# A hybrid decoder layer: early products added by PE, sums by ACT and accumulating transfers, w_down's sums and the h reload moved

## The chip, the core and the metric

The kernel runs on one core of one Trainium2 chip. The metric is the device time of one execution in microseconds. All arithmetic is float32 to the caller; products go through PE as pairs of float32r numbers, a high part and a rest.

## What is computed

One decoder layer on 1024 tokens of width 1024: two token mixers (dilated-window attention and stick-breaking attention), gated and added, then cross-attention to 256 memory tokens, then a gated MLP with a width-3 convolution, then a norm. The change touches how the last parts are carried out.

```python
h = h + (gate_a * ya + gate_b * yb) @ w_out
h = h + memory_cross_attn(rms_norm(h), rms_norm(mem), w_xq, w_xkv, w_xo)
u = rms_norm(h) @ w_up                      # 1024 x 5632
u = causal_conv3(u) + conv_b
h = h + (silu(u[:, :2816]) * u[:, 2816:]) @ w_down
return rms_norm(h)
```

## The kernel before

Every matrix product takes three matmuls of 128x512 outputs (`mm3`, lines 97 to 99): high by high, high by rest, rest by high. A weight arrives raw by SP's queue (`raw_w`, line 70); ACT copies it to the high part (line 80) and DVE subtracts to get the rest (line 81).

The two large products of the MLP use a scheme with seven block products in place of eight. Tokens are cut in two halves (block column 1 is tokens 0 to 511), and the contraction in two halves. For `w_up`, `right_sums` (852) builds sums of the normed activations once (t1 to t4), and `sum_weights` (909) builds sums of the two weight blocks on DVE for each of 22 output tiles g. For each g the products add up in two PSUM banks, A and B. The results are put together as ug (gate) and uv (value), each a tile of 1026 columns: two leading zeros and 1024 tokens.

Two of the seven products, `11` and `21`, need only the first token half. For g under 10 (`NEARLY`) `up_early` (824) computes them beforehand, three of them between the second attention half and its output product, seven behind: p1 is the first product, c11 the sum of both; both are stored in DRAM (`e_d`). In the loop over g `up_start` (889) loads w_up's two tiles, p1, and c11 into ug; `up_middle` (925) and `up_end` (949) do the other five products and add p1 on DVE wherever it belongs:

```python
nc.vector.tensor_tensor(u["U2"], u["A"], u["p1"], op=ALU.add)                      # 936
nc.vector.tensor_tensor(u4, u["A"], u["p1"], op=ALU.add)                           # 944
nc.vector.tensor_tensor(u["uv"][:, 2 + HT:2 + T], u["B"], u4, op=ALU.add)          # 947
nc.vector.tensor_tensor(c12, u["A"], u["p1"], op=ALU.add)                          # 955
nc.vector.tensor_tensor(u["uv"][:, 2:2 + HT], u["B"], u["U2"], op=ALU.add)         # 959
```

For g from 10 on, all seven products are done in the loop, ACT copies p1, U2, U4 and c12 out of bank A, and DVE does the adds with bank D and bank B. Bank B holds t3's product at first, is read for the second half of uv, and goes on with t4's product for the first half. Then for ug and uv ACT starts y (965), DVE adds two convolution taps (966, 967), ACT applies silu, DVE multiplies (972), and for every second g DVE makes four sums (982 to 988). Seven tiles per pair go to DRAM as `r_d` from POOL's queue. ug and uv share two buffers (tag `hu`), so the tiles of one g become free only when the taps of the g before are done.

`down` (991) is the same scheme for `w_down`: seven runs of 11 steps kg, each with 12 matmuls and two loads of 256 KB on SP's queue (1014, 1015), one from `r_d`, one of a weight. Three of the runs take sums of weight blocks. These sums (`sd_d`) don't depend on the input activations; they are made in DRAM alone by `weight_sums` (512): for each of 11 pairs four copies of 256 KB on SP's queue (`put`, 516) and three accumulating transfers on POOL's queue (`add`, 519), each waiting for the one before. `sum_step` (533) issues them piece by piece; it is called in the loop over the merged gates (634), in `tok_gemm` (574), `feat_gemm` (733), `up_early` (825), `up_middle` (926) and `up_end` (950). h was stored to DRAM (`spill_h`, 836) to free its tiles, and `loads` (1001) reads it back after the first run of `down`, eight tiles of 512 KB and the gain gF on POOL's queue, into the tiles of ug, uv and y of the last outputs.

The order on each engine and queue comes from a scheduler, which goes by program order and by a simulated time line. `keep_in_program_order` pins a transfer to its place. Each engine and each queue then runs in that fixed order, and a waiting instruction holds all behind it.

Of the kernel before, what the change touches and what calls it, by code (L numbers as in the profile page):

```python
# [7 lines left out]
F32 = mybir.dt.float32  # L8
F32R = mybir.dt.float32r
AF = mybir.ActivationFunctionType  # L10
# [32 lines left out]
def hybrid_layer(ctx: ExitStack, tc: tile.TileContext, x, xT, mem, memT, w_in, w_v, w_br, w_out, w_xq, w_xk, w_xv, w_xo, w_up,  # L43
# [9 lines left out]
    vec = cp.tile([P, V_N], F32, name="vec")  # L53
    neghalf = cp.tile([P, 16], F32, name="neghalf")

    ga_d = dp.tile([16, P, T], F32, name="ga_d")
# [4 lines left out]
    r_d = dp.tile([NF // 2, 7, P, HT], F32, name="r_d")  # L61
    e_d = dp.tile([NEARLY, 2, P, HT], F32, name="e_d")
    h_d = dp.tile([8, P, D], F32, name="h_d")
# [98 lines left out]

    nc.sync.dma_start(ident, consts[:, 0:P])
    nc.sync.dma_start(cst, consts[:, P:])
    rs8 = ap.tile([P, 8], F32, name="rs8")
    for t in range(8):
# [14 lines left out]
    def load_rs_perm():  # L181
        rs_perm[4] = ap.tile([P, 16], F32, name="rs_p1")[:, 0:8]
        rs_perm[16] = ap.tile([P, 8], F32, name="rs_p2")
# [349 lines left out]
    def sum_step():  # L533
        n = sums_n[0]
        sums_n[0] += 1
        for b, ops in enumerate(sums):
            d = n - 15 * b // 2
            if 0 <= d < 12 and d % 2 == 0:
                ops[d // 2]()
# [5 lines left out]
    for p in range(NA + NS):  # L545
        units = [(dil_step, (8 * p + i,)) if p < NA else (sb_unit, (p, i)) for i in range(8)]
        if p == NA:
            units[CPOS:CPOS] = [(combine, (0,)), (combine, (1,))]
            units = [(dil_step, (8 * NA + i,)) for i in range(3)] + units
        gemms = [(fn, ()) for fn in proj_pair(p + 1)] if p + 1 < NA + NS else []  # L550
        ng = len(gates) if p == NA + NS - 1 else GATES[p]
        for _ in range(ng):
            gemms.append((gate, (gates.pop(0),)))
        nu, ngm = len(units), len(gemms)
        if p == NA + NS - 1:
            ngm = TAIL_MIX
        k = 0
        for u, (fn, a) in enumerate(units):
            while k < ngm and k * nu <= u * ngm:
                gemms[k][0](*gemms[k][1])  # L560
                k += 1
            fn(*a)
        while k < len(gemms):
            gemms[k][0](*gemms[k][1])
            k += 1
# [5 lines left out]
    def tok_gemm(th, ch, nkg, wdram, lhs, done):  # L571
        ps = quad("mmt")
        for kg in range(nkg):
            sum_step()
            ws = list(wchunks(wdram[ch, kg]))
            lh = [lhs(2 * kg + kk) for kk in range(2)]
            for t in range(4):
                ts_ = slice(t * P, (t + 1) * P)
                for kk in range(2):
                    lhi, llo = lh[kk]  # L580
                    mm3(ps[t], (lhi[:, ts_], llo[:, ts_]), ws[kk][1:], kg == 0 and kk == 0, kg == nkg - 1 and kk == 1)
        for t in range(4):
            done(4 * th + t, ch, ps[t])
# [80 lines left out]

    def etile(name):
        return ep.tile([P, HT], F32, tag="e", name=name, bufs=7)

# [16 lines left out]
    def mem_prep():  # L684
# [10 lines left out]
        rsm = xp.tile([P, 2], F32, name="rsm")  # L695
        for t in range(2):
# [35 lines left out]
    def feat_gemm(ps, dram, n2):  # L732
        sum_step()
        for k0, wh, wl in wchunks(dram):
            for kk in range(4):
                k, ks = k0 + kk, slice(kk * P, (kk + 1) * P)
                mm3(ps, (wh[:, ks], wl[:, ks]), (n2[0][:, k], n2[1][:, k]), k == 0, k == NK - 1)
# [85 lines left out]

    def up_early(g):
        sum_step()
        l11, l12 = gate_weights(g)
        pa, pb = bank("mm", 3, "pe"), bank("mm", 3, "pe")
        p1, c11 = etile("p1"), etile("c11")
        product(pa, l11, R["11"], True)
        nc.scalar.activation(p1, pa, AF.Copy)  # L830
        product(pb, l12, R["21"], True)
        nc.vector.tensor_tensor(c11, pb, p1, op=ALU.add)
        nc.gpsimd.dma_start(e_d[g, 0], p1)
        nc.gpsimd.dma_start(e_d[g, 1], c11)

# [53 lines left out]
    def up_start(g):  # L889
        u = {}  # L890
        u["ug"], u["uv"] = (htile([P, 2 + T + 14], "hu", n) for n in ("ug", "uv"))
        for n in ("ug", "uv"):
            nc.gpsimd.memset(u[n][:, 0:2], 0.0)
        u["A"] = bank("zz", 2, "pA")
        u["w1"] = raw_w(w_up[g])
        u["w2"] = htile([P, 2 * HT], "hr", "w2")
        nc.sync.dma_start(u["w2"], w_up[NF + g])
        u["p1"] = etile("p1")
        if g < NEARLY:
            nc.sync.dma_start(u["p1"], e_d[g, 0])  # L900
            nc.sync.dma_start(u["ug"][:, 2:2 + HT], e_d[g, 1])
        else:
            hi, lo = split(u["w1"])
            u["l12"] = hi[:, HT:], lo[:, HT:]
            product(u["A"], (hi[:, :HT], lo[:, :HT]), R["11"], True)
            nc.scalar.activation(u["p1"], u["A"], AF.Copy)
        return u

    def sum_weights(u):
# [15 lines left out]
    def up_middle(g, u):  # L925
        sum_step()
        early = g < NEARLY
        if not early:
            d = bank("mm", 3, "pD")
            product(d, u["l12"], R["21"], True)  # L930
            nc.vector.tensor_tensor(u["ug"][:, 2:2 + HT], d, u["p1"], op=ALU.add)
        s1, s2, s3, u["s4"] = sum_weights(u)
        product(u["A"], s2, R["t2"], early)
        u["U2"] = etile("U2")
        if early:
            nc.vector.tensor_tensor(u["U2"], u["A"], u["p1"], op=ALU.add)
        else:
            nc.scalar.activation(u["U2"], u["A"], AF.Copy)
# [4 lines left out]
        if early:  # L943
            nc.vector.tensor_tensor(u4, u["A"], u["p1"], op=ALU.add)  # L944
        else:
            nc.scalar.activation(u4, u["A"], AF.Copy)
        nc.vector.tensor_tensor(u["uv"][:, 2 + HT:2 + T], u["B"], u4, op=ALU.add)

    def up_end(g, u):
        sum_step()  # L950
        early = g < NEARLY
        product(u["A"], u["s4"], R["22"], False)
        c12 = u["ug"][:, 2 + HT:2 + T]
        if early:
            nc.vector.tensor_tensor(c12, u["A"], u["p1"], op=ALU.add)
        else:
            nc.scalar.activation(c12, u["A"], AF.Copy)
        product(u["B"], u["l22"], R["t4"], False)
        nc.vector.tensor_tensor(u["uv"][:, 2:2 + HT], u["B"], u["U2"], op=ALU.add)
        ys = []  # L960
# [30 lines left out]
    def down():  # L991
# [14 lines left out]
        def run(ps, i, first):  # L1006
            for kg in range(KG):
# [30 lines left out]

        run(A, 1, True)
        loads()  # L1040
        into(A, 0, 0, ALU.add)
        B = [bank("zz", 2, "dB") for _ in range(2)] + [bank("tr", 2, "dB") for _ in range(2)]
        run(B, 2, True)
        into(B, 0, 0, ALU.add, 0)
        run(A, 6, False)
        into(A, 0, 1, ALU.subtract)
        run(B, 7, True)
        into(B, 1, 1, ALU.subtract)
        run(A, 5, False)
        into(A, 1, 1, ALU.subtract, 0)  # L1050
# [21 lines left out]
    o1 = x_att(1, q1)  # L1072
    for g in range(3):
        up_early(g)
    xo_half(1, o1)
# [10 lines left out]
    ncw = mp.tile([P, 144], F32, name="ncw")  # L1086
    nc.vector.tensor_scalar(ncw[:, :3 * NF], vec[:, V_CW + 3 * NF:V_CW + 6 * NF], -1.0, None, op0=ALU.mult)
# [91 lines left out]
```

## Time and profile before

| what | us |
|---|---|
| median of 3 runs | 1793.84 |
| lowest and highest | 1786.63 and 1794.06 |
| the profiled execution | 1791.09 |
| its span in the trace | 1789.3 |
| busy PE, DVE, ACT, POOL | 1696.2, 1156.3, 823.3, 265.7 |

The stages in the span: projections and dilated attention to some 440 us, stick-breaking from there to 730, gates and merge to 840, `w_out` and cross-attention to 1090, early products and activation sums to 1157, the loop over g to 1548, then `down`. PE is the matmul engine, DVE the vector engine, ACT the scalar engine, POOL GpSimd, SP the engine that only issues transfers. A matmul's busy time in the trace is longer than its distance to the next one, since they overlap; the distance is what counts. The granted clock is the share of 2.4 GHz that PE was given.

### The profile page before, as it was taken

The numbers are of one execution on the slowest core, as the hardware profiler recorded it, in microseconds if no ns is written. First come the engines' busy times: TensorE is split into PE (matmuls) and PEld (weight loads), VectorE is DVE, ScalarE is ACT, GpSimd is POOL, SyncE is SP. The second block draws the span as 40 slices with busy tenths as digits, with TensorE's granted clock in tenths as the row PEclk, the third lists the DMA queues.
The fourth block names the chain that finished last, engine by engine and source line by source line (L and its number), as shares of the span: only waits on it lengthen the run. The fifth ranks groups of instructions, "written<-read, shape, count | busy, mean of one in ns | idle before, by whom it ended". The sixth has DMA issues, their size and how long they took to land.

```text
span 1789.3 us, 23340 instructions
## 1 busy us (share of the span) xinstructions
PE 1696.2 (95%) x8578; PEld 1377.3 (77%) x8578; DVE 1156.3 (65%) x1823; ACT 823.3 (46%) x1398; POOL 265.7 (15%) x434
## 2 busy tenths in 40 slices
PE   7999999998999999999899989799899999889996
PEld 5977777877878788787788777577688888668885
DVE  3664655367757566475545664999888788735556
ACT  5454554455345445344444454443344454424344
POOL 0442333211100000001100112111111111200002
PEclk9999999999999999999999999899999999989998
DMA  8443323323413122666652654566563432566663
GB/s 303 111 128 88 111 78 84 98 70 96 137 53 101 54 77 68 196 206 242 159 151 85 173 139 163 184 176 194 172 160 120 120 123 72 219 238 191 190 194 134
DMA packets 93650, 253.06 MB, mean 141 GB/s; under 512 B 14752, under 2 KB 15008, under 8 KB 93536
## 3 DMA queue, kind: packets, MB, share of 16 engines
q1 hardware_dynamic: 65360, 164.58, 28.5%
q0 software_dynamic: 28176, 86.99, 17.9%
q8 instruction: 67, 1.10, 0.3%
q14 instruction: 47, 0.39, 0.1%
HBM read 186.15 MB, written 71.67 MB: 144 GB/s over the span
## 4 chain that ended last, share of the span: by engine, by line
PE 40%; DVE 5%; DMA 4%; ACT 1%; issue 1%; POOL 1%; SPq 0%; POOLq 0%; DVEq 0%; ACTq 0%
PE pA L97 3%; PE pA L98 3%; PE pA L99 3%; PE dA L97 2%; PE dA L99 2%; PE dA L98 2%; PE mmt L97 2%; PE mmt L98 2%; PE dB L97 2%; PE mmt L99 2%; PE dB L99 2%; PE dB L98 2%; PE pB L98 2%; PE pB L97 2%; PE pB L99 2%; DMA sd_d<-in_w_down_dram 1%
## 5 line engine op out<-in xcount | busy, mean ns | idle before, releaser
L99 PE MATMUL mm<-a2h,wl 128*128 128x512 f32 x592 | 234.1, 396 | 0.0
L98 PE MATMUL mm<-a2l,wh 128*128 128x512 f32 x592 | 233.7, 395 | 0.0
L97 PE MATMUL mm<-a2h,wh 128*128 128x512 f32 x592 | 233.6, 395 | 0.0
L81 DVE TENSOR_TENSOR wl<-wr,wh 128x1024 fp32r<-128x1024 f32 (+1 forms) x119 | 145.2, 1221 | 91.2 <-ACT wh L80 90.8
L80 ACT ACTIVATE wh<-wr 128x1024 fp32r<-128x1024 f32 (+1 forms) x119 | 124.1, 1044 | 147.5 <-PE mmv L99 29.7
L81 DVE TENSOR_TENSOR dl<-rl,dh 128x1024 fp32r<-128x1024 f32 x77 | 94.2, 1223 | 94.7 <-ACT dh L80 91.0
L80 ACT ACTIVATE dh<-rl 128x1024 fp32r<-128x1024 f32 x77 | 81.5, 1059 | 124.9 <-PE dA L99 44.7
L98 PEld LDWEIGHTS mm<-a2l,wh 128*128 128x128 f32 x592 | 111.7, 189 | 22.2 <-issue 0.9
L99 PEld LDWEIGHTS mm<-a2h,wl 128*128 128x128 f32 x592 | 111.8, 189 | 22.0 <-issue 1.0
L97 PEld LDWEIGHTS mm<-a2h,wh 128*128 128x128 f32 x592 | 111.8, 189 | 21.8 <-issue 0.9
L490 DVE TENSOR_TENSOR_SCAN kp<-kp 128x128 f32<-128x128 f32 (+7 forms) x64 | 86.7, 1355 | 26.9 <-ACT kp L487 26.7
L487 ACT ACTIVATE kp<-zz,zsc 128x512 f32<-128x512 f32 (+3 forms) x96 | 55.6, 583 | 49.1 <-DVE zz L486 44.4
L378 ACT ACTIVATE sp<-sp,nm 128x128 f32<-128x128 f32 (+1 forms) x96 | 42.4, 442 | 73.1 <-DVE nm L376 73.0
L97 PE MATMUL pA<-a2h,mh 128*128 128x512 f32 x176 | 71.8, 408 | 3.2 <-DVE U L944 2.8
L499 ACT ACTIVATE at<-tra 128x512 f32<-128x512 f32 (+3 forms) x96 | 43.1, 489 | 68.6 <-PE tra L497 68.4
L97 PE MATMUL dA<-dh 128*128 128x512 f32 x176 | 63.3, 401 | 11.2 <-ACT dh L80 11.2
L98 PE MATMUL dA<-dl,dh 128*128 128x512 f32 x176 | 71.4, 406 | 1.8 <-DVE dl L81 1.8
L99 PE MATMUL dA<-dh,dl 128*128 128x512 f32 x176 | 71.2, 404 | 0.0
L98 PE MATMUL pA<-a2l,mh 128*128 128x512 f32 x176 | 70.9, 403 | 0.0
L99 PE MATMUL pA<-a2h,ml 128*128 128x512 f32 x176 | 70.6, 401 | 0.0
L110 POOL TENSOR_TENSOR ss<-ss,neghalf 128x1 f32<-128x1 f32 x24 | 25.1, 1124 | 254.7 <-DVE ss L593 253.6
L488 ACT ACTIVATE gg<-zz,zsc 128x512 f32<-128x512 f32 (+3 forms) x96 | 55.8, 583 | 6.8 <-DVE gg L491 6.7
(347 smaller groups left out, 4512.1 us busy)
## 6 DMA issues: line engine op xcount, KB each, us to landing
rl<-r_d SPq DMA_DIRECT2D x77, 256.0 KB, 2.7
wr<-in_w_in_dram SPq DMA_DIRECT2D x37, 512.0 KB, 3.9
wr<-in_w_up_dram SPq DMA_DIRECT2D x32, 512.0 KB, 4.5
w<-in_w_up_dram SPq DMA_DIRECT2D x22, 512.0 KB, 3.3
r_d<-ts POOLq DMA_DIRECT2D x44, 256.0 KB, 3.5
rl<-sd_d SPq DMA_DIRECT2D x44, 256.0 KB, 3.2
r_d<-y POOLq DMA_DIRECT2D x33, 256.0 KB, 3.8
rl<-in_w_down_dram SPq DMA_DIRECT2D x33, 256.0 KB, 3.1
```

The lines of the kernel that those rows point to most:

```text
L80: nc.scalar.activation(hi, raw, AF.Copy)
L81: nc.vector.tensor_tensor(lo, raw, f(hi), op=ALU.subtract)
L97: nc.tensor.matmul(ps, wh, rh, start=first, stop=False, **kw)
L98: nc.tensor.matmul(ps, wh, ro, start=False, stop=False, **kw)
L99: nc.tensor.matmul(ps, wo, rh, start=False, stop=last, **kw)
L110: nc.gpsimd.tensor_tensor(ss, ss, neghalf[:, :n], op=ALU.pow)
L378: nc.scalar.activation(sp[:, a, :n], sp[:, a, :n], AF.Exp, scale=0.125, bias=nm[:, a:a + 1], accum_out=ost[:, 130 + a:131 + a])
L487: nc.scalar.activation(kp[:, c0:c1], z[:, :n], AF.Sigmoid, scale=zsc[:, 1, i:i + 1])
L488: nc.scalar.activation(gg[:, c0:c1], z[:, :n], AF.Sigmoid, scale=zsc[:, 0, i:i + 1])
L490: nc.vector.tensor_tensor_scan(rev, rev, rev, 1.0, op0=ALU.mult, op1=ALU.bypass)
L499: nc.scalar.activation(s[:, :nb * P], tp[:, :nb * P], AF.Copy)
```

## The change

- `sum_step` is called in the units of the stick-breaking phase (pairs 6 to 9) and still in the merge loop, no longer in the later places. The sums of one pair start every 3 calls, before every 7.5.
- `up_early` takes two outputs at a time. The first product is stored as a high part and a rest (`er_d`, float32r) and the second product adds to it in the same PSUM bank; c11 is a copy of that bank by ACT. Two outputs are computed between the second attention half and its output product, eight behind.
- In the loop, for g under 10, the early product is loaded as its two parts by POOL's queue, and PE adds it into bank A with two matmuls by the identity. The adds of p1 on DVE are gone; U2, U4 and c12 are copies by ACT for all g.
- Bank B (and bank D) is copied into uv (ug) by ACT, and U4, U2 (p1) are added by an accumulating transfer from SBUF to SBUF on POOL's queue (`add_into`).
- The two leading zeros and the load of c11 move from `up_start` to `up_middle`.
- h is read back in quarters of four loads of 256 KB, on SP's queue, at kg 3 to 6 of four of the runs; gF in a fifth.
- Some small tiles get more columns.

```diff
+    ident_r = cp.tile([P, P + 16], F32R, name="ident_r")[:, :P]
...
-    e_d = dp.tile([NEARLY, 2, P, HT], F32, name="e_d")
+    e_d = dp.tile([NEARLY, P, HT], F32, name="e_d")
+    er_d = dp.tile([NEARLY, 2, P, HT], F32R, name="er_d")
...
+    nc.scalar.activation(ident_r, ident, AF.Copy)
...
-            d = n - 15 * b // 2
+            d = n - 3 * b
...
             fn(*a)
+            if p >= NA:
+                sum_step()
...
-            sum_step()
...
-    def up_early(g):
-        sum_step()
-        l11, l12 = gate_weights(g)
-        pa, pb = bank("mm", 3, "pe"), bank("mm", 3, "pe")
-        p1, c11 = etile("p1"), etile("c11")
-        product(pa, l11, R["11"], True)
-        nc.scalar.activation(p1, pa, AF.Copy)
-        product(pb, l12, R["21"], True)
-        nc.vector.tensor_tensor(c11, pb, p1, op=ALU.add)
-        nc.gpsimd.dma_start(e_d[g, 0], p1)
-        nc.gpsimd.dma_start(e_d[g, 1], c11)
+    def up_early(gs):
+        ps = {}
+        for g in gs:
+            ps[g] = bank("mm", 3, "pe"), *gate_weights(g)
+            product(ps[g][0], ps[g][1], R["11"], True)
+            hi, lo = etile("phi", F32R), etile("plo", F32R)
+            hilo(hi, lo, ps[g][0])
+            nc.gpsimd.dma_start(er_d[g, 0], hi)
+            nc.gpsimd.dma_start(er_d[g, 1], lo)
+        for g in gs:
+            product(ps[g][0], ps[g][2], R["21"], False)
+            c11 = etile("c11")
+            nc.scalar.activation(c11, ps[g][0], AF.Copy)
+            nc.gpsimd.dma_start(e_d[g], c11)
...
-        u["p1"] = etile("p1")
         if g < NEARLY:
-            nc.sync.dma_start(u["p1"], e_d[g, 0])
-            nc.sync.dma_start(u["ug"][:, 2:2 + HT], e_d[g, 1])
+            hi, lo = etile("phi", F32R), etile("plo", F32R)
+            nc.gpsimd.dma_start(hi, er_d[g, 0])
+            nc.gpsimd.dma_start(lo, er_d[g, 1])
+            nc.tensor.matmul(u["A"], ident_r, hi, start=True, stop=False, skip_group_check=True)
+            nc.tensor.matmul(u["A"], ident_r, lo, start=False, stop=True, skip_group_check=True)
...
+    def add_into(dst, ps, x):
+        nc.scalar.activation(dst, ps, AF.Copy)
+        nc.gpsimd.dma_start(dst, x, accum_op=ALU.add)
...
     def up_middle(g, u):
-        sum_step()
-        early = g < NEARLY
-        if not early:
+        for n in ("ug", "uv"):
+            nc.gpsimd.memset(u[n][:, 0:2], 0.0)
+        if g < NEARLY:
+            nc.sync.dma_start(u["ug"][:, 2:2 + HT], e_d[g])
+        else:
             d = bank("mm", 3, "pD")
             product(d, u["l12"], R["21"], True)
-            nc.vector.tensor_tensor(u["ug"][:, 2:2 + HT], d, u["p1"], op=ALU.add)
+            add_into(u["ug"][:, 2:2 + HT], d, u["p1"])
...
-        nc.vector.tensor_tensor(u["uv"][:, 2 + HT:2 + T], u["B"], u4, op=ALU.add)
+        nc.scalar.activation(u4, u["A"], AF.Copy)
+        add_into(u["uv"][:, 2 + HT:2 + T], u["B"], u4)
...
-        nc.vector.tensor_tensor(u["uv"][:, 2:2 + HT], u["B"], u["U2"], op=ALU.add)
+        add_into(u["uv"][:, 2:2 + HT], u["B"], u["U2"])
...
-        def loads():
-            nc.gpsimd.dma_start(gF, bass.AP(tensor=ln_f.tensor, offset=ln_f.offset, ap=[[0, P], [1, D]]))
-            for t in range(8):
-                tc.keep_in_program_order(nc.gpsimd.dma_start(h[t], h_d[t]))
+        def load_h(th, ch):
+            hs = slice(ch * HT, (ch + 1) * HT)
+            return [lambda t=t: nc.sync.dma_start(h[t][:, hs], h_d[t][:, hs]) for t in range(4 * th, 4 * th + 4)]
...
+                if kg >= 3 and kg - 3 < len(also):
+                    tc.keep_in_program_order(also[kg - 3]())
...
-    for g in range(3):
-        up_early(g)
+    up_early((0, 1))
...
-    for g in range(3, NEARLY):
-        up_early(g)
+    for g in range(2, NEARLY, 2):
+        up_early((g, g + 1))
```

## Rows read from the trace of the kernel before

**Rows 1.** The page, part 1: busy time, share and instructions of each engine.

```profile
PE 1696.2 (95%) x8578; PEld 1377.3 (77%) x8578; DVE 1156.3 (65%) x1823; ACT 823.3 (46%) x1398; POOL 265.7 (15%) x434
```

**Rows 2.** Stretches: span, busy (count) of PE/PEld/DVE/ACT/POOL, clock, DMA share, GB/s.

```profile
500.00:700.00 200.00, 200.00 (x1195) 160.28 (x1194) 129.05 (x161) 100.98 (x194) 10.14 (x19) 1.00 0.21 68
...
1139.00:1157.00 18.00, 9.60 (x30) 6.73 (x28) 16.37 (x21) 4.75 (x5) 1.69 (x4) 0.72 0.59 220
1157.00:1300.00 143.00, 129.63 (x529) 100.32 (x529) 130.50 (x159) 54.22 (x52) 23.10 (x51) 0.98 0.60 175
1300.00:1540.00 240.00, 240.00 (x1040) 195.21 (x1039) 198.89 (x225) 113.00 (x134) 32.09 (x76) 1.00 0.40 118
1546.00:1594.00 48.00, 34.98 (x125) 26.21 (x124) 23.11 (x22) 15.26 (x15) 7.49 (x14) 0.82 0.79 295
1600.00:1750.00 150.00, 150.00 (x658) 123.15 (x657) 80.25 (x85) 65.92 (x79) 0.57 (x1) 1.00 0.62 191
```

**Rows 3.** Waits of PE from 840 to 1300 us: total, times, longest.

```profile
PE pA L97 <- ACT mh L80: 16.4, 9, 6.1
PE pk L99 <- DVE wl L81: 6.0, 2, 5.2
```

**Rows 4.** Timeline of SP's queue and of DVE, 1270 to 1283 us.

```profile
1276.47 0.48 SPq L516 DMA_DIRECT2D sd_d<-sd_d  x1
1277.00 0.59 SPq L900 DMA_DIRECT2D p<-e_d  x1
...
1282.10 0.69 DVE L936 TENSOR_TENSOR U<-pA,p 128x512 f32<-128x512 f32 x1 [3.33 <-DMA p<-e_d]
```

**Rows 5.** The chain that ended last, 1545 to 1580 us: start, duration, what.

```profile
1550.63 1.29 DVE y L966
...
1552.19 9.34 DMA rl<-in_w_down_dram
...
1561.55 12.30 DMA rl<-in_w_down_dram
```

**Rows 6.** DMA issues of the whole run: transfer, queue, count, KB, median us to landing.

```profile
rl<-in_w_down_dram SPq DMA_DIRECT2D x33, 256.0 KB, 3.1
...
sd_d<-in_w_down_dram SPq DMA_DIRECT2D x22, 256.0 KB, 4.9
sd_d<-in_w_down_dram POOLq DMA_DIRECT2D x11, 512.0 KB, 8.0
...
sd_d<-in_w_down_dram POOLq DMA_DIRECT2D x22, 256.0 KB, 5.9
kh<-kh POOLq DMA_DIRECT2D x20, 256.0 KB, 3.7
...
h<-h_d POOLq DMA_DIRECT2D x8, 512.0 KB, 8.8
```

**Rows 7.** DVE, 1157 to 1300 us: one group, and two rows of the timeline.

```profile
L936 DVE TENSOR_TENSOR U<-pA,p 128x512 f32<-128x512 f32 x10 | 6.9, 686 | 4.1 <-DMA p<-e_d 3.9 <-PE pA L99 0.2
...
1251.37 1.27 DVE L966 SCALAR_TENSOR_TENSOR y<-uv,ncw,y 128x1024 f32<-128x1024 f32 x1
...
1253.77 1.27 DVE L967 SCALAR_TENSOR_TENSOR y<-uv,ncw,y 128x1024 f32<-128x1024 f32 x1
```

**Rows 8.** ACT's timeline: y of uv (early output); copy of ug (last).

```profile
1249.15 1.25 ACT L965 ACTIVATE y<-uv,vec,ncw 128x1024 f32<-128x1024 f32 x1 [0.47 <-DVE uv L959]
...
1544.54 0.60 ACT L957 ACTIVATE ug<-pA 128x512 f32<-128x512 f32 x1 [1.75 <-PE pA L99]
```

**Rows 9.** Line 519, the accumulating transfers of w_down's sums.

```profile
DMA to landing us min/median/max: 4.2/7.1/11.1
```

**Rows 10.** The chain that ended last, 850 to 872 us.

```profile
860.78 5.03 DMA sd_d<-sd_d
...
866.32 0.81 POOL sd_d L519
...
869.88 0.58 PE pk L99
```

More of the change, by code (lines that the diff above doesn't have):

```diff
@@ L163, in hybrid_layer @@
     nc.sync.dma_start(ident, consts[:, 0:P])
+    nc.scalar.activation(ident_r, ident, AF.Copy)
     nc.sync.dma_start(cst, consts[:, P:])
-    rs8 = ap.tile([P, 8], F32, name="rs8")
+    rs8 = ap.tile([P, 16], F32, name="rs8")[:, 0:8]
     for t in range(8):
@@ L182, in load_rs_perm @@
         rs_perm[4] = ap.tile([P, 16], F32, name="rs_p1")[:, 0:8]
-        rs_perm[16] = ap.tile([P, 8], F32, name="rs_p2")
+        rs_perm[16] = ap.tile([P, 32], F32, name="rs_p2")[:, 0:8]
         for r in range(4):
@@ L663, in htile, with etile @@
         return hpool.tile(shape, dt, tag=tag, name=name, bufs=HBUFS[tag])
-    def etile(name):
-        return ep.tile([P, HT], F32, tag="e", name=name, bufs=7)
+    def etile(name, dt=F32):
+        return ep.tile([P, HT], dt, tag="e", name=name, bufs=7)
     h = []
@@ L694, in mem_prep @@
                 hilo(mh[c][:, kk], ml[c][:, kk], mr[:, kk], vec[:, g:g + 1])
-        rsm = xp.tile([P, 2], F32, name="rsm")
+        rsm = xp.tile([P, 18], F32, name="rsm")[:, :2]
         for t in range(2):
@@ L891, in up_start @@
         u["ug"], u["uv"] = (htile([P, 2 + T + 14], "hu", n) for n in ("ug", "uv"))
-        for n in ("ug", "uv"):
-            nc.gpsimd.memset(u[n][:, 0:2], 0.0)
         u["A"] = bank("zz", 2, "pA")
@@ L905, in up_start @@
             product(u["A"], (hi[:, :HT], lo[:, :HT]), R["11"], True)
+            u["p1"] = etile("p1")
             nc.scalar.activation(u["p1"], u["A"], AF.Copy)
         return u
+    def add_into(dst, ps, x):
+        nc.scalar.activation(dst, ps, AF.Copy)
+        nc.gpsimd.dma_start(dst, x, accum_op=ALU.add)
     def sum_weights(u):
@@ L925, in up_middle @@
     def up_middle(g, u):
-        sum_step()
-        early = g < NEARLY
-        if not early:
+        for n in ("ug", "uv"):
[3 more added lines that the diff above has]
+        else:
             d = bank("mm", 3, "pD")
             product(d, u["l12"], R["21"], True)
-            nc.vector.tensor_tensor(u["ug"][:, 2:2 + HT], d, u["p1"], op=ALU.add)
+            add_into(u["ug"][:, 2:2 + HT], d, u["p1"])
         s1, s2, s3, u["s4"] = sum_weights(u)
-        product(u["A"], s2, R["t2"], early)
+        product(u["A"], s2, R["t2"], False)
         u["U2"] = etile("U2")
[L935 to L938, printed above, removed]
+        nc.scalar.activation(u["U2"], u["A"], AF.Copy)
         u["B"] = bank("tr", 2, "pB")
@@ L942, in up_middle @@
         u4 = etile("U4")
[L943 to L946, printed above, removed]
-        nc.vector.tensor_tensor(u["uv"][:, 2 + HT:2 + T], u["B"], u4, op=ALU.add)
+        nc.scalar.activation(u4, u["A"], AF.Copy)
+        add_into(u["uv"][:, 2 + HT:2 + T], u["B"], u4)
     def up_end(g, u):
-        sum_step()
-        early = g < NEARLY
         product(u["A"], u["s4"], R["22"], False)
[L953 to L957, printed above, removed]
+        nc.scalar.activation(u["ug"][:, 2 + HT:2 + T], u["A"], AF.Copy)
         product(u["B"], u["l22"], R["t4"], False)
-        nc.vector.tensor_tensor(u["uv"][:, 2:2 + HT], u["B"], u["U2"], op=ALU.add)
+        add_into(u["uv"][:, 2:2 + HT], u["B"], u["U2"])
         ys = []
@@ L999, in down, with run @@
             h[t] = htile([P, D], HTAGS[t], "h")
-        def loads():
-            nc.gpsimd.dma_start(gF, bass.AP(tensor=ln_f.tensor, offset=ln_f.offset, ap=[[0, P], [1, D]]))
-            for t in range(8):
-                tc.keep_in_program_order(nc.gpsimd.dma_start(h[t], h_d[t]))
-        def run(ps, i, first):
+        def load_h(th, ch):
+            hs = slice(ch * HT, (ch + 1) * HT)
+            return [lambda t=t: nc.sync.dma_start(h[t][:, hs], h_d[t][:, hs]) for t in range(4 * th, 4 * th + 4)]
+        def run(ps, i, first, also=()):
             for kg in range(KG):
@@ L1037, in out_half @@
                     nc.sync.dma_start(out[t * P:(t + 1) * P, c:c + HT], ft[:, c:c + HT])
-        run(A, 1, True)
-        loads()
+        run(A, 1, True, load_h(0, 0))
         into(A, 0, 0, ALU.add)
         B = [bank("zz", 2, "dB") for _ in range(2)] + [bank("tr", 2, "dB") for _ in range(2)]
-        run(B, 2, True)
+        run(B, 2, True, load_h(0, 1))
         into(B, 0, 0, ALU.add, 0)
-        run(A, 6, False)
+        run(A, 6, False, load_h(1, 1))
         into(A, 0, 1, ALU.subtract)
-        run(B, 7, True)
+        run(B, 7, True, [lambda: nc.sync.dma_start(gF, bass.AP(tensor=ln_f.tensor, offset=ln_f.offset,
+                                                                ap=[[0, P], [1, D]]))])
         into(B, 1, 1, ALU.subtract)
-        run(A, 5, False)
+        run(A, 5, False, load_h(1, 0))
         into(A, 1, 1, ALU.subtract, 0)
@@ L1085, in hybrid_layer @@
     tp_ = ts_.enter_context(tc.tile_pool(name="tp", bufs=1, side="right"))
-    ncw = mp.tile([P, 144], F32, name="ncw")
+    ncw = mp.tile([P, 160], F32, name="ncw")
     nc.vector.tensor_scalar(ncw[:, :3 * NF], vec[:, V_CW + 3 * NF:V_CW + 6 * NF], -1.0, None, op0=ALU.mult)
```

## The prediction, made before the changed kernel was run

> **What bounds the kernel now.** The page's first part says TensorE (PE): busy for 95% of the span, with 8578 matmuls [rows 1]. A busy share can't tell a full engine from a stretched one, so next I read the table by stretches for the number of matmuls. In 1600 to 1750 us, the steady part of `down`, PE ran 658 matmuls in 150 us, 0.228 us each [rows 2]; that is my price of a 128x512 matmul. Against it, three stretches that the change touches are short. From 1157 to 1300 us (the first outputs g of the up loop, those with early products) 529 matmuls should take 120.6 us and took 143: 22.4 us lost. From 1546 to 1594 us (start of `down`) 125 matmuls should take 28.5 and took 48: 19.5 lost. From 1139 to 1157 us (before the up loop) 30 should take 6.8 and took 18: 11.2 lost [rows 2]. From 1300 to 1540 us 1040 matmuls need 237 of 240 us: nothing can be won there, it can only be lost. In the two holes the granted clock averages 0.82 and 0.72 [rows 2]: some matmuls after the idle time ran at the lower of the two levels, 1.2 GHz. That is part of the loss, and goes with the hole.
>
> Who bounds the short stretches? In 1157 to 1300 us DVE is busy 130.5 of 143 us [rows 2], PE's waits name `mh`, the weight splits that follow DVE's sums [rows 3], and the timeline shows why DVE itself stops: SP's put of `sd_d` issues only at 1276.47 us, after an accumulating transfer, the load of p1 stands behind it at 1277.00, and DVE's add of U starts at 1282.10 after 3.33 us idle [rows 4]. In 1546 to 1594 us DMA moves 295 GB/s, and the chain is two loads of w_down of 9.34 and 12.30 us [rows 2, 5], against a median of 3.1 [rows 6].
>
> **The h reload in quarters.** Before, eight h loads of 512 KB [rows 6] and gF (128x1024 words) go out around the first product of `down`: 4.7 MB of the 14.2 MB that 295 GB/s move in those 48 us. Now four quarters of 256 KB (1.05 MB) stand there, the rest in later runs, which move 191 GB/s with PE full [rows 2]; one more MB in 30 us makes it 226, under the 295 seen. 3.67 MB less at 295 GB/s is 12.4 us. It can't give more than 19.5; it gives nothing if the quarters, now on SP among the weight loads, wait for the tiles of the last up output and hold those loads behind them. I take **12.4**. Late next: r_d of the last pair, which run A needs only for its last kg.
>
> **The early loop.** Its 529 matmuls at 60 per output are 8.8 outputs, so 16.2 us each. DVE loses five adds per output (U2, U4, ug, uv twice), 0.68 to 0.69 us each [rows 7], 0.60 from start to start in a queue: 3.0 of its 14.8 us (130.5 over 8.8), leaving 11.8. PE gets two identity matmuls: 62 at 0.228 is 14.1, the new floor. ACT gets five copies of 0.60 us [rows 8], 3.0 on top of its 54.22 us over 8.8, 6.2 [rows 2]: covered. POOL gets two loads of the early sum and two adds, 3.2 us at 0.81 per issue [rows 10], on top of 23.1 us over 8.8; SP loses the p1 load and all the `sd_d` puts.
>
> But a new wait closes a ring. The second product into bank B can't start before ACT has copied the first half of uv out, that copy needs the uv tile of the output before, and that tile is free when its two DVE steps are done. From the end of the product: copy 0.60, the accumulating transfer L, ACT's y 1.25, two DVE steps of 1.28 (2.48 back to back), copy 0.60, product 12 x 0.228 = 2.74 [rows 7, 8], six handoffs at some 0.1: 8.3 + L. L is in no row. From below the POOL copy kh, SBUF to SBUF with 256 KB, 3.7 us; from above the adds of 256 KB in DRAM, 5.9 [rows 6], and the longest add, 11.1 [rows 9]. The copy has the same memory, the add the same operation; I take 5.0 between them: 13.3. DVE is a queue in order: of uv's two steps the second began at 1253.77 after the first at 1251.37, 1.2 later than back to back, and the first 1.0 after ACT's y had ended [rows 7, 8]; DVE will be less full, so I add 1.7 of these 2.2. So 15.0 per output, and 8.8 x 1.2 = **10.6** won; ends: 18.5 won (PE's floor), and with L at 11.1 a period of 21.1, 43 lost.
>
> The Trainium skill, "DMA: Bandwidth & Descriptors", Anatomy of one DMA, fits a POOL transfer as 2.0 us plus its bytes at 436 GB/s; estimated from that page L would be 2.6, the ring under the floor, and the sum 1755. Both rows of this size speak against it (3.7 and 5.9).
>
> The later outputs have 84 matmuls, 19.15 us, above the ring: no cost while L is under 9.1; an add into ug comes a product earlier than it is needed.
>
> **w_down's sums.** In the stretch 840 to 872 us an add on POOL waited for a put, the norm's rstd stood behind it, DVE's weight split behind that, and PE waited until 869.88 [rows 10]: 5.2 us in one wait [rows 3]. The list of PE's waits has no second one of that kind. I take **5** won (0 to 8). The puts in the up loop are counted above. Moved into stick-breaking are nearly all of 44 puts on SP and 33 adds on POOL, 22 MB written. Hiding it: from 500 to 700 us DMA is busy 0.21 and POOL 10 us of 200 [rows 2], and a sum's steps stand two units (some 16 us) apart where an add lands in 5.9 to 8.0 [rows 6]. If the cover fails, a put on SP waits with w_in loads behind it, two buffers deep; PE is full there, so each delay counts. I take **2** lost (0 to 26, rival 4).
>
> **Early products before the loop.** PE's count is the same. DVE's sum becomes a subtraction of one size, ACT gets a copy. One early output (24 matmuls, 5.5 us) moves from the second attention half behind `xo_half`, towards the hole of 11.2 us; its old place loses filler. The second product now waits for DVE's read of the bank, and DVE is busy 16.4 of 18 us there [rows 2]; the pair's other product covers 2.7. I take **2** won (-4 to 5.5). The copy of the identity, the memsets and the padded tiles: nothing; idle ACT and POOL cover them, and uncovered they are under 1 us.
>
> **Sum.** 12.4 + 10.6 + 5 - 2 + 2 = 28. The profiled execution took 1791.09 us (span 1789.3); 28 less is 1763. The median of the runs is 2.75 above it, their spread 7.4; I say **1764**.
>
> **Rivals.**
> 1. PE's floor: L is the copy's 3.7, so the ring is 12.0 + 1.7 = 13.7, under 14.1, and the early loop gains 18.5: 1755, with the h reload at its best 1748. For: DMA's load falls as the sums leave. Chance 0.14.
> 2. The add costs two copies, since it reads both sides: L = 7.4, period 17.4. The early loop then loses 10.6: 1791.1 - 17.4 + 10.6 = 1784; at L = 6.2 it gains nothing: 1774. The Trainium skill, "Collectives: The Full Stack", The bandwidth ceiling, has this rule: an add reads two sources and runs at half the copy's rate. The rows show 5.9 for an add against 4.9 for a put of the same 256 KB [rows 6], 1.2 times. Chance 0.14.
> 3. The quarters wait on SP for tiles and hold the weight loads: no gain at `down`: 1776. For: the chain enters that wait through DVE's steps on the last y [rows 5]. Chance 0.08.
> 4. The sums don't vanish but stop stick-breaking instead: a put on SP behind a late add, a weight load behind the put. If five of the eleven pairs cost what the one wait did, 5.2, it is 26 in place of 2: 1787, no change. Against: DMA and POOL are little used there [rows 2]. Chance 0.14.
> 5. Slower: L as the ring's long link, in the up loop. It decides from L = 8.2: 8.8 x (8.2 + 10.0 - 16.2) equals the 17.4 won elsewhere. At 10, 8.8 x 3.8 + 12 x 0.85 = 44 lost: 1817. For: the longest add took 11.1; against: those wrote DRAM while DMA was full. Chance 0.12.
>
> **How the numbers follow.** The forecast has 0.38. Faster by over 0.5% (what a measurement of this kernel can tell from no change, 9 us) are the forecast and rivals 1 to 3: 0.74; within it is rival 4: 0.14; slower is rival 5: 0.12. The range goes from 1742, near the best ends of all terms, to 1789, the end of rival 4; outside lies rival 5 and little else.
>
> **What would show it.** Right: about 15 us between the first pA matmuls of early outputs, DVE under 85% there; no add of `sd_d` after 850 us; no w_down load over 6 us at the start of `down`; accumulating transfers landing in 4 to 6 us. Wrong: ACT's y of uv waiting long for a transfer while PE waits for ACT's copy of uv (rivals 2, 5); an h quarter on SP with a long wait before it (3); `wh` waiting for w_in loads in stick-breaking (4).

## The result and the profile after

The changed kernel takes **1781.89 us** (median of 7; 1780.32 to 1787.86) against 1793.84 (7): ratio 0.9944, 95% interval 0.9925 to 0.9963. The forecast was 1764; its range, 1742 to 1789, held. The sign was right and the gain was less than half: 12 us in place of 28. The profiled execution took 1780.45 us, 10.7 less in span. Four marks that both timelines have divide it: the first matmul with t3's low part for output 0 (the "first t3 product" below), the same for output 9, the end of the loop's last product, the end.

| stretch | before | after | won | forecast |
|---|---|---|---|---|
| start to first t3 product | 1150.5 | 1148.9 | 1.6 | 5 - 2 + 2 = 5 |
| nine early outputs | 149.9 | 152.3 | -2.4 | 10.6 |
| to the loop's last product | 246.8 | 245.8 | 1.0 | 0 |
| from there to the end | 242.1 | 231.6 | 10.5 | 12.4 |

Of the 17.3 us that are missing in span, the nine early outputs lack 13.0; they failed, and the first stretch won little. The page's first part, beside [rows 1]:

```profile
PE 1693.4 (95%) x8598; PEld 1378.1 (77%) x8598; DVE 1113.0 (63%) x1737; ACT 871.0 (49%) x1495; POOL 326.9 (18%) x511
```

DVE has 43 us less to do, ACT 48 and POOL 61 more, and little came of it. By stretches, in the columns of [rows 2]:

```profile
500.00:700.00 200.00, 195.01 (x1157) 155.78 (x1154) 125.45 (x158) 97.22 (x188) 25.87 (x37) 0.98 0.57 126
1139.00:1157.00 18.00, 14.22 (x48) 10.69 (x47) 9.70 (x13) 5.40 (x8) 3.74 (x7) 0.81 0.59 182
1157.00:1300.00 143.00, 128.13 (x540) 101.69 (x539) 106.16 (x114) 77.11 (x97) 41.32 (x78) 0.99 0.65 184
1300.00:1540.00 240.00, 240.00 (x1045) 195.73 (x1044) 178.06 (x185) 132.71 (x172) 57.05 (x105) 1.00 0.52 141
1546.00:1594.00 48.00, 40.65 (x164) 31.70 (x163) 27.21 (x27) 18.50 (x19) 3.51 (x6) 0.93 0.84 285
```

In the early loop DVE fell from 130.5 to 106.2 of 143 us, and TensorE still did no more: 540 matmuls where an output now has 62, so 8.7 outputs against 8.8. DVE had been nearly full (91%) and is no longer what bounds. The waits of PE from 840 to 1300 us name what does, beside [rows 3]:

```profile
PE pA L99 <- ACT U L953: 14.9, 8, 3.2
PE pe L101 <- DVE wl L83: 5.6, 1, 5.6
...
PE pB L99 <- ACT mh L82: 2.0, 1, 2.0
```

The wait on `mh` went and one on ACT's copy of U4 came; the 5.2 us for `pk` went and one of 5.6 for an early product came. (`pA` is bank A, `pe` a bank of the early products, `mh` and `wl` the high part and the rest of a weight tile; L953 copies U4.) One output of the early loop, ACT first and then PE:

```profile
1220.23 1.25 ACT L966 ACTIVATE y<-uv,vec,ncw 128x1024 f32<-128x1024 f32 x1 [2.04 <-DMA uv<-U]
1221.98 1.06 ACT L82 ACTIVATE mh<-w 128x1024 fp32r<-128x1024 f32 x1 [0.50 <-PE pA L100]
1222.94 0.58 ACT L953 ACTIVATE U<-pA 128x512 f32<-128x512 f32 x1
```

```profile
1221.78 0.39 PE L101 MATMUL pA<-a2h,ml 128*128 128x512 f32 x1
1223.57 0.50 PE L99 MATMUL pA<-a2h,mh 128*128 128x512 f32 x1 [1.41 <-ACT U L953]
```

s1 and s4 are two of the weight sums of an output; their products stand one behind the other in bank A. The first PE row is the last matmul of s1, the second the first of s4. ACT copies the bank out between, and only after it has split a weight tile (`mh`) that s1's matmul just before set free. No other product of TensorE's order stands there.

### The profile page after: what moved, and what is told of

It is laid out like the page before. It is cut to its first block, busy times and chain, and to the rows that moved or that the text cites. A ratio compares the mean times of both kernels' runs of the same rounds, so it can differ in the third digit from the quotient of the medians.

```text
span 1778.6 us, 23614 instructions
## 1 busy us (share of the span) xinstructions
PE 1693.4 (95%) x8598; PEld 1378.1 (77%) x8598; DVE 1113.0 (63%) x1737; ACT 871.0 (49%) x1495; POOL 326.9 (18%) x511
## 4 chain that ended last, share of the span: by engine, by line
PE 66%; issue 13%; DMA 10%; DVE 5%; ACT 3%; POOL 3%; SPq 0%; POOLq 0%; DVEq 0%; ACTq 0%
PE mm L99 4%; PE mm L101 4%; PE mm L100 4%; PE pA L99 3%; PE pA L100 3%; PE pA L101 3%; DMA sd_d<-in_w_down_dram 2%; DMA uv<-U 2%; PE mmt L99 2%; PE dA L100 2%; PE dA L101 2%; PE mmt L100 2%; PE mmt L101 2%; PE dA L99 2%; DMA xw<-xs 2%
## 5 line engine op out<-in xcount | busy, mean ns | idle before, releaser
L99 PE MATMUL pA<-a2h,mh 128*128 128x512 f32 x176 | 70.5, 400 | 14.9 <-ACT U L953 14.9
```

Of the source, the lines that this page charges most:

```text
L99: nc.tensor.matmul(ps, wh, rh, start=first, stop=False, **kw)
```

## The experiments

**The parts alone.** The change has three: the sums, the quarters of h, and the third part (early products by TensorE, copies by ACT, accumulating transfers). Five kernels leave parts out. The times are medians, and each ratio is against runs of before on the same chip. The last three columns of the table come from the one profiled execution of each kernel; that of `sums_only` took 1787.09 us, 6.5 above its median.

`sums_only`, the kernel before with the calls of the sums as in the change:

```diff
-            d = n - 15 * b // 2
+            d = n - 3 * b
...
             fn(*a)
+            if p >= NA:
+                sum_step()
```

> The kernel before with w_down's sums moved into stick-breaking alone. Forecast: 5 won at the first pk and 2 lost in stick-breaking, plus what the puts and adds cost in the up loop, counted with the early loop: 1788 to 1791. What the two traces show so far: +4 to +5 at the end of stick-breaking, -11 from there to the cross-attention, so -6 there, and an early loop freed of sd_d puts that won 3 to 8 us: 1780 to 1787. The rival, that the sums cost in stick-breaking what they cost later: within 3 us of the kernel before.

`h_only`, the kernel before with the quarters:

```diff
-        run(A, 1, True)
-        loads()
+        run(A, 1, True, load_h(0, 0))
```

> The kernel before with the reload of h in quarters alone. My forecast's term: the start of the last stage (first bank B product of it less the loop's last pA) shortens by 12.4 us: 1781.5. What the two traces show so far is 9 us: 1785. The rival, that quarters on SP hold the weight loads as much as they free: within 2 us of the kernel before, 1792 to 1796.

`sums_h`, both of these edits:

> The kernel before with two of the three parts of the change: the sums of w_down in stick-breaking and the reload of h in quarters; the early products, ACT's copies and the accumulating transfers are left out. Each part alone gave 0.994 to 0.995 of before. Theory D (the third part, for which I forecast 12.6 us won, loses in truth about 8, since the early outputs with DVE's adds need 15.9 us each once the sums are gone and 16.9 with the change): the two add up to 19-20 us, 1771 to 1775, faster than the changed kernel by 7 to 11 us. The rival, that the sums and the quarters win the same time twice (the same loads at the start of the last stage): 1778 to 1783.

`early_only`, the changed kernel with both undone:

> The kernel before with the third part alone: early products added by TensorE, copies by ACT, accumulating transfers; the sums of w_down where they were and h reloaded whole. My forecast: 12.6 us won less what the sums' puts give back, 1781 to 1786. Theory D: no gain, 1793 to 1803, with early outputs of 16 us or more from TensorE's 62 matmuls and the wait between s1 and s4.

`no_h`, the changed kernel with the second undone:

> The changed kernel with h reloaded whole, as before: the sums and the third part alone. If the quarters are worth their 9 us here too: 1789 to 1793. If the third part alone already frees the start of the last stage (with the third part and no quarters, the time from the up loop's last product to the end was 231.7 us, as short as the changed kernel's 231.6, against 242.1 before), the quarters win nothing in the changed kernel: 1779 to 1784.

| kernel | us | ratio, interval | first t3 | nine outputs | last product to end |
|---|---|---|---|---|---|
| sums_only | 1780.57 | 0.9939, 0.9921 to 0.9958 | 1152.3 | 143.0 | 243.2 |
| h_only | 1784.65 | 0.9948, 0.9926 to 0.9970 | 1151.0 | 154.1 | 232.6 |
| sums_h | 1772.32 | 0.9891, 0.9864 to 0.9918 | 1147.3 | 142.7 | 232.6 |
| early_only | 1816.58 | 1.0137, 1.0109 to 1.0166 | 1165.1 | 168.0 | 231.7 |
| no_h | 1784.89 | 0.9942, 0.9921 to 0.9963 | 1152.3 | 153.0 | 233.0 |
| the change | 1781.89 | 0.9944, 0.9925 to 0.9963 | 1148.9 | 152.3 | 231.6 |

Theory D held: **without the third part the change is 9.6 us faster** (1772.3 against 1781.9, the intervals apart). The sums win 11 alone and the quarters 9, and together 20; on top of both, the third part costs 9.1 us of span, 9.6 of them in the nine early outputs. And it wins what the quarters win: it alone shortens the way from the last product to the end from 242.1 to 231.7, so that quarters on top of it (the change against `no_h`) win 1.4 us there, and the intervals of the two show no difference. I had expected `early_only` at no gain and at most 10 lost; it loses 24: 15 us before the loop, 18 in the nine outputs, 3 in the later ones, 10 won back at the end. In the loop its transfers stand on POOL's queue among the adds of `sd_d`, and the wait for U4 grows. PE's waits from 1140 to 1330 us, and a row of ACT:

```profile
PE pA L99 <- ACT U L955: 24.9, 8, 5.1
```

```profile
1222.78 1.24 ACT L969 ACTIVATE y<-uv,vec,ncw 128x1024 f32<-128x1024 f32 x1 [6.35 <-DMA uv<-U]
```

The early loop of `sums_h` is DVE's: 138.4 of 143 us, with 561 matmuls at 60 per output, 15.3 us each (15.9 over the nine outputs of the table, the slow first one among them). [Rows 2] had 529 there.

```profile
1157.00:1300.00 143.00, 133.60 (x561) 104.26 (x562) 138.38 (x168) 57.86 (x56) 17.57 (x48) 1.00 0.43 150
```

**What bounds the early outputs of the change.** `u4_dve` and `t4_kept`:

```diff
-        nc.scalar.activation(u4, u["A"], AF.Copy)
+        if g < NEARLY:
+            nc.vector.tensor_copy(u4, u["A"])
+        else:
+            nc.scalar.activation(u4, u["A"], AF.Copy)
```

> The changed kernel, but in the early outputs U4 is copied out of bank A by DVE and no longer by ACT. Theory A (a ring through ACT's queue): in the changed kernel U4's copy stands on ACT behind the y of the output before, which waits for the accumulating transfer; TensorE's s4 product waits for U4, and the t4 product, whose copy starts the next accumulating transfer, stands behind s4. From y to y that is 10.4 us plus the landing, 5.2 to 5.6, together the 16.0 us seen. With U4 on DVE the ring is the forecast's 8.3 us plus the landing, so 14.1 to 14.6 us from output to output, the waits of pA for ACT's U (14.9 us) go, and the time falls by 10 to 15 us from 1781.9, to 1767-1772. Theory B (the forecast's own ring, with a landing or a queueing of 7.7 in all in place of 6.7): the period stays at 16.0, and the time within 3 us of 1782. Theory C (the w_up loads arrive late, DVE stands idle before its weight sums): the period stays near 16, DVE's wait for w_up stays at 13 us or grows, and the time stays within 4 us of 1782.

```diff
-        product(u["A"], u["s4"], R["22"], False)
-        nc.scalar.activation(u["ug"][:, 2 + HT:2 + T], u["A"], AF.Copy)
         product(u["B"], u["l22"], R["t4"], False)
         add_into(u["uv"][:, 2:2 + HT], u["B"], u["U2"])
+        product(u["A"], u["s4"], R["22"], False, keep=g < NEARLY)
+        nc.scalar.activation(u["ug"][:, 2 + HT:2 + T], u["A"], AF.Copy)
```

> The changed kernel with the two last products of an output swapped: t4 (bank B) before s4 (bank A), held in that order for the early outputs; ACT still copies U4. Theory A: s4's 2.8 us leave the ring, TensorE does t4 while ACT copies U4, so the period falls from 16.0 to 14.2-14.8 and the time by 8 to 14 us, to 1768-1774; TensorE then waits before t4 for ACT's copy of bank B, under 2 us per output. Theory B: t4 already starts when its bank is copied, so the swap gives nothing in the ring and puts s4 after it: the period stays at 16 or more, 1782 to 1790. Theory C: no change, 1778 to 1786.

`adds_dve`:

```diff
-        nc.scalar.activation(dst, ps, AF.Copy)
-        nc.gpsimd.dma_start(dst, x, accum_op=ALU.add)
+        nc.vector.tensor_tensor(dst, ps, x, op=ALU.add)
```

> The changed kernel with the accumulating transfers of the up loop taken out: DVE adds bank B and U2, bank B and U4, and pD and p1, as before the change; the early product is still added by TensorE and U2, U4 and ug are still copied by ACT. Theories A and B: the landing (5 us) leaves the ring, DVE gets 2 adds of 0.6 us per output, so DVE has about 13 us per output and TensorE's floor of 14.1 us sets the period: 14.1 to 14.6, 12 to 17 us less than the changed kernel, 1765 to 1770, unless the later outputs lose. Theory C (w_up loads): less DMA traffic by 0.5 MB per output, a few us won at most, 1775 to 1782.

Measured: 1778.86, 1784.74 and 1816.89 us. Theory A as I had put it fell: U4 on DVE shortens the shortest period (from an output's first t3 product to the next one's) from 16.0 to 15.4, but its nine outputs take 152.3 us as in the change; t4 first turns the wait into one for the copy of bank B, and no period is under 16.5, as theory B had it. PE's waits from 1148 to 1305 us in the three kernels:

```profile
PE pA L99 <- DVE U L954: 12.9, 8, 3.1
```

```profile
PE pB L99 <- ACT uv L917: 15.1, 8, 2.1
```

```profile
PE pA L99 <- ACT U L952: 12.7, 9, 1.5
```

The third is the telling one. Without any accumulating transfer the early outputs of `adds_dve` come every **16.0 us, eight times in a row**, with 1.4 to 1.5 us of waiting for U4 in each. So 16.0 is no ring through a transfer (theory B): it is 62 matmuls, 14.4 us, and the turnaround of bank A. (Its 35 us lost lie in the later outputs, where TensorE's order came out otherwise: periods of 17.9 and 25 to 28 us in turn, against 19.3. So this run gives no price of the adds.) Theory A2 follows: put a product on bank B between any two on bank A. `woven`, and `woven9` with the tenth output in the old order (`keep` holds a product behind the one emitted before it):

```diff
+        product(u["A"], s2, R["t2"], False, keep=True)
...
+            up_last(g - 1, last)
+        product(u["A"], s1, R["t1"], False, keep=True)
...
+        product(u["B"], s3, R["t3"], True, keep=True)
...
+        product(u["A"], s4, R["22"], False, keep=True)
```

> The changed kernel with another order of TensorE's products in the early outputs, held there: t2 of this output, t4 of the one before, s1, t3, s4. So a product on bank B stands between any two on bank A, and none waits for a copy that has only just begun. Theory A2 (each early output of the changed kernel is TensorE's 62 matmuls, 14.4 us, and 1.4 to 1.6 us of waiting between s1 and s4 for a copy behind which nothing stands; the transfers cost only the slower outputs): the waits of pA for U (14.9 us) fall under 4, the period goes to 14.4-15.0 us, and the time falls 9 to 15 us, to 1767-1773. Theory B (the accumulating transfer's ring sets 16): t4 comes a product later than now, so the period stays at 16 to 18: 1780 to 1800. Theory C (w_up loads late): 15 to 16 us, 1775 to 1782.

> The changed kernel with the woven order for the first nine early outputs only, the tenth in the order of the change, so that the seam to the later outputs is the changed kernel's. In the woven kernel the outputs came every 14.3 to 15.2 us, but 25.5 us and a wait of 3.9 us for ACT's weight split at the seam took most of it back. If the seam was the order's fault: the wait of 3.9 us goes, 1769 to 1773. If the ring of the last accumulating transfers makes the seam, whatever the order: 1775 to 1779.

1776.93 (0.9918, 0.9890 to 0.9945) and 1776.96 us. Seven of `woven`'s nine periods are 14.3 to 15.2 us, the others 16.2 and 17.8, and the waits for U4 from 14.9 to 0.7. PE's waits of `woven`, 1148 to 1325 us:

```profile
PE pA L906 <- DMA phi<-er_d: 4.9, 3, 2.4
PE pA L99 <- ACT wh L82: 3.9, 1, 3.9
PE pA L907 <- DMA plo<-er_d: 1.3, 3, 0.8
PE pA L99 <- ACT U L963: 0.7, 1, 0.7
```

A2 is right on the period and promised too much of the time: nine outputs take 137.3 us, 15 less than in the change, but their first t3 product stands 9 us later in this order, and the seam to the eleventh output takes 25.5 us in place of 19.3. At the eleventh output's t3 product the two kernels are level (1320.6 and 1320.5 us); the 3 us of span that `woven` keeps come later, and its interval overlaps that of the change. `woven9` has the same seam (25.0), so the order of the tenth output does not make it; what does stayed open.

The Trainium skill, "Perfetto Trace Analysis", Optimizing Tensor Performance, has the rule that A2 uses: let independent groups of matmuls take turns on different banks, so that the copy out of one runs beside the next. These rows agree: 14.9 us of waits for U4 in the early outputs without, 0.7 with.

**The first stretch.** `early3` and `sums_spread`:

```diff
-    up_early((0, 1))
+    up_early((0, 1, 2))
```

> The changed kernel with three early products ahead of the second cross-attention output, as before the change, and not two. If the early part lost its forecast gain because the product moved behind xo_half finds DVE full with the sums of the ffn's right halves, and left a hole where it was, the first pB comes 2 to 5 us earlier and the time falls to 1777-1780. If DVE's work alone sets the first pB, whatever TensorE does, there is no change: 1780 to 1784.

```diff
-            d = n - 3 * b
-            if 0 <= d < 12 and d % 2 == 0:
-                ops[d // 2]()
+            d = n - 6 * b
+            if 0 <= d < 18 and d % 3 == 0:
+                ops[d // 3]()
```

> The changed kernel with the sums of w_down begun earlier and spread wider: a step after each unit of the dilated heads too, and three units between the steps of a sum in place of two. If the 4 to 5 us lost in stick-breaking come from several adds that POOL issued together at 573 us, whose landing (16.3 us) held the stores and puts behind them, the 5.2 us wait at 615 us goes and stick-breaking ends 4 to 5 us earlier: 1777. If the sums' traffic itself costs, wherever it stands, the loss moves into the dilated heads (7 us puts and adds between q, k loads): 1780 to 1786. If it is only the number of writes: no change, 1780 to 1784.

`early3`: 1780.75, no change; the wait for `wl` stays in it (5.5 us). `sums_spread`: 1802.71, and the loss did move into the dilated heads (the first transpose of stick-breaking starts at 404 us in place of 368, the last ends at 758 in place of 732). The cost of the sums in stick-breaking itself shows in the change at 572 to 615 us, rows of POOL, then one of ACT:

```profile
571.57 0.55 POOL L513 DMA_DIRECT2D yt_d<-ye  x1 [10.04 <-DVE ye L512]
572.11 3.44 POOL L522 DMA_DIRECT2D sd_d<-in_w_down_dram  x4
574.76 1.35 POOL L229 DMA_DIRECT2D ga_d<-xr  x1
575.33 1.66 POOL L522 DMA_DIRECT2D sd_d<-in_w_down_dram  x1
597.60 0.82 POOL L522 DMA_DIRECT2D sd_d<-in_w_down_dram  x1 [20.62 <-DMA sd_d<-sd_d]
608.21 0.81 POOL L522 DMA_DIRECT2D sd_d<-in_w_down_dram  x1 [9.79 <-DMA sd_d<-sd_d]
608.74 0.85 POOL L229 DMA_DIRECT2D ga_d<-xr  x1
609.30 0.84 POOL L513 DMA_DIRECT2D yt_d<-ye  x1
```

```profile
614.91 0.28 ACT L502 ACTIVATE at<-tra 128x128 f32<-128x128 f32 x1 [9.94 <-DMA yt_d<-ye]
```

Five adds that stood behind one store go out together, the next waits for a put, the next store of `ye` stands behind that, and `at` waits for the tile of `ye`. PE lost 5.0 us there, and 4.4 to 6.3 us in each of the ten others that have the sums in that place with the change's spacing and POOL's store, and nothing in the three that have them later. `yt_act` gives that store to another queue:

```diff
-            nc.gpsimd.dma_start(yt_d[2 + p - NA, :, (i // 4) * HT:(i // 4 + 1) * HT], ye)
+            nc.scalar.dma_start(yt_d[2 + p - NA, :, (i // 4) * HT:(i // 4 + 1) * HT], ye)
```

> The changed kernel with the store of ye in stick-breaking issued by ACT in place of POOL, so that it no longer stands behind adds that wait for puts. If that queue makes the 5.2 us wait at 615 us (seen in all seven kernels with the sums in stick-breaking, in neither without): the wait goes, stick-breaking ends 4 to 6 us earlier, 1775 to 1779. If the DMA engines are simply full with the five adds of 572 to 576 us: the store is late all the same, 1780 to 1785; ACT stopping before the store for DVE's copy would show as an idle time of ACT before yt_d.

1773.82 us (0.9899, 0.9873 to 0.9925), and not for the reason I gave. The wait at 615 us went and one of 7 us came at 549, behind a transfer of the chain that ended last:

```profile
533.85 13.29 DMA ga_d<-xr
```

Stick-breaking ends no earlier (734.8 us). The time came back in the early loop, 5 of the 6.6 us of span: eight periods of 16.0, nine outputs in 147.2 us, although from the up loop on each engine has the changed kernel's instructions in its order. ACT's wait there from 1150 to 1300 us, in the change and in `yt_act`:

```profile
ACT y L966 <- DMA uv<-U: 15.1, 7, 3.9
```

```profile
ACT y L966 <- DMA uv<-U: 4.0, 5, 1.2
```

Three last kernels: the change once more (`after_again`), and ACT's store with `woven` and with `sums_h`.

> The changed kernel as it is, once more, beside two others on the same chip. In the yt_act kernel all five engines had the same instructions in the same order from the up loop on, and its early outputs came every 16.0 us where the changed kernel's profile showed 16.9 on average. If that was chance of one execution: 16.0 to 17.0 here, and about 1780. If it belongs to the program: again four or five of its nine early periods between 16.7 and 19.3, and 1780 to 1784.

> The changed kernel with the woven order in the early outputs and the store of ye issued by ACT. If the two add up (5 and 8 us): 1767 to 1770. Theory D2 (the third part of the change can win only where its order leaves no wait between s1 and s4): early outputs of 14.3 to 14.6 us, and a seam of at most 22 us if the accumulating transfers land in 4.6 us as in yt_act; then it comes within 5 us of the next kernel. If yt_act's gain was the early loop's alone, woven has it already: 1774 to 1777.

> The kernel before with the sums in stick-breaking, h in quarters, and the store of ye issued by ACT; nothing of the third part. If ACT's store wins its 8 us in stick-breaking and w_out: 1764 to 1767, the fastest of all. If its 8 us came from the early loop's transfers, which this kernel does not have: 1771 to 1774.

1781.57 (0.9935, 0.9913 to 0.9956), 1774.27 (0.9900, 0.9877 to 0.9924) and **1769.81** us (0.9888, 0.9857 to 0.9919). The change repeats its long early periods (17.2, 20.9, 19.0 us) in a second trace, of an execution of 1791.93 us, so they were not the chance of one execution; of `yt_act` there is one trace. `woven` and the store do not add up. The store is worth 2.5 us to `sums_h`, between my two ranges and within its intervals: the fastest is the change without its third part, 1770 to 1772.

## Why the prediction was wrong

**The early loop** is the step that failed: "8.8 x 1.2 = 10.6 won" was 2.4 us lost over nine outputs. Three errors are in it. First, the base. The 16.2 us per output were not DVE's work alone; part was the hole that [rows 4] show, where a load of p1 stands behind a put of `sd_d`. I counted SP's loss of the puts in this term, but the sums win that time alone: 149.9 us for the nine outputs become 142.7 in `sums_h`, so 7 of the 10.6 were theirs (one trace each; `h_only`, with before's early loop, took 154.1). Second, "62 at 0.228 is 14.1, the new floor": TensorE's order leaves 1.4 to 1.6 us of waiting between s1 and s4, so its floor in that order is 16.0 (`adds_dve`, `yt_act`); `woven`, without the wait, reaches 14.3. I looked for a ring through bank B and did not follow bank A, whose copy the change moves from DVE to ACT, behind `mh` and behind the y that waits for the transfer. Third, where transfers land late, ACT's y waits and U4's copy behind it: 5.1 us more in the change than in `yt_act` (152.3 against 147.2), which is itself 4.5 above `sums_h`: 9.6 lost in nine outputs. Why they land late there is open. L itself was about right: 5.0 forecast, 4.7 measured (median of 44; 5.4 in 1160 to 1290 us).

```profile
uv<-U POOLq DMA_DIRECT2D x44, 256.0 KB, 4.7
...
kh<-kh POOLq DMA_DIRECT2D x20, 256.0 KB, 3.9
```

Most of the signs that I named for "right" came nevertheless: DVE at 74%, the last transfer into `sd_d` issued at 755 us, the adds landing in 4.7, one load of w_down of 6.3 us and none longer. Only the period did not (16.9 us on average). Each of the others says that an engine or a queue is free, and none what TensorE waits for. Of the signs against it half came: y of uv waited 15.1 us for transfers, but TensorE for the copy of U4, not of uv.

**The h reload** was right in place and a little large: 10.5 us in the change and 9.5 in `h_only` (242.1 less 232.6) for 12.4. The stretch is not empty without these bytes: it still moves 285 GB/s. Nor was 295 GB/s, by which I divided, a limit: the same 48 us of `early_only` moved 341. The loads of w_down left the chain, and in their place stand the last accumulating transfer and its y:

```profile
1545.91 6.41 DMA uv<-U
...
1554.03 1.24 ACT y L966
...
1556.68 1.28 DVE y L967
```

What I did not see is that the third part wins the same time without it (`early_only`, `no_h`), so the 10.5 us of the change can't be put down to the quarters alone. The traces have a reason that fits, and no run tests it: in `early_only` seven of h's eight loads go out 15 to 27 us after the loop's last product, in the kernel before 8 to 21, and TensorE's waits at the start of `down` fall from 13.0 us to 6.3.

**The sums**: 5 won and 2 lost forecast. From `h_only` to `sums_h`, the first product behind stick-breaking (bank `pa`) comes 6.5 us later (rival 4's mechanism, once: 4.4 us of PE in one wait); from there to cross-attention's first value product (`pv`) 13.3 us are won, where [rows 10] are, but more than the 8 at which I had ended the term. Of these, 10.0 lie behind the first matmul into `pk`: I had priced the wait alone (5.2 us), but the granted clock was 0.86 in 860 to 885 us, part of it at the lower level, and is 1.00 there in `sums_h`. The first t3 product comes 3.7 us earlier, near the 3 that the two terms make, but by luck: both were too small, and 3 us are lost again before the loop. With the early loop the sums are worth 11, the best part of the change. (Four runs of `down` read them, not three: `rl<-sd_d` has 44 loads.)

**Early products**: 2 won forecast. From `sums_h` to the change the first t3 product is 1.6 us later; the hole of [rows 2] became the wait for `wl` behind DVE's sums, and `early3` shows that the moved product is not its cause. "DVE is busy" was the right worry: in DVE's order there, sums of activations stand ahead of that split.

**The rivals.** 1: the floor was 16.0, not 14.1. 2 and 5: L was 4.7, so neither. 3: the quarters won 9 alone. 4: about 6 us, between my 2 and its 26.

The Trainium skill, "Collectives: The Full Stack", The bandwidth ceiling, has an add at half the copy's rate, and says it of the reduce step of a collective. The transfers here do not show it: 4.7 us for an add against 3.9 for a copy of the same size. Nor do they show the 2.6 us that I estimated from the Trainium skill, "DMA: Bandwidth & Descriptors", Anatomy of one DMA.

## What to carry to other kernels

Freeing a full engine is worth what the next bound leaves: before pricing a move, list for each bank the product, the copy and the product again, and see what TensorE has between. A period that is the same to a tenth of a microsecond need not be a ring: here it was work plus a turnaround. Test a ring by taking its long link out. And price parts of a change against each other: here one part's gain lay in another's hole, and two parts won the same time.

## What was not expected of the hardware

Transfers landed at another pace in two kernels that differ only in the queue of one store far back in the program: in 1160 to 1290 us the loads of w_up into `wr` landed in 6.0 us (median) in the change and 4.3 in `yt_act`, the accumulating ones in 5.4 and 4.6, with the same instructions in the same order. The second trace of the change has 5.7 and 5.2 in the same part of the loop. Why is open, and so is which came first, the late transfers or the long periods. And the adds that went out together in stick-breaking landed late: in 571 to 600 us those of 256 KB took 11.2 us against 7.2 in the whole run. Other transfers of that stretch were late too (13.5 us for a load of w_in, 4.2 in the whole run), so it is not shown that the adds slow each other.

```profile
sd_d<-in_w_down_dram POOLq DMA_DIRECT2D x4, 256.0 KB, 11.2
```
